# Row operations of a two-block transformer moved to GpSimd, and the planner that orders them

## The chip, the cores and the metric

One core of one Trainium2 chip. The metric is the device time of one execution in microseconds (us), the median of several runs. The engines are TensorE (PE; its weight loads are PEld), VectorE (DVE), ScalarE (ACT), GpSimd (POOL) and SyncE (SP), which issues most of the DMAs.

## What is computed

Two transformer blocks follow one another, on 256 tokens of width 1024, in float32. The first is attention plus an mLSTM and a gated feed-forward layer. The second begins with a layer norm of `x` (gain and bias from `emb_ln_g`, `emb_ln_b`). Its mixer joins two branches, a spatial gating unit and an RWKV-7 recurrence:

```
x = layer_norm(x, emb_ln_g, emb_ln_b)
mod = silu(c) @ w_ada + b_ada            # sh1, sc1, gt1, sh2, sc2, gt2
h = x * (1.0 + sc1) + sh1
p = h @ w_in
u, v = gelu(p[:512]), layer_norm(gelu(p[512:1024]), sg_ln_g, sg_ln_b)
y_a = u * (w_s_masked @ v + b_s)         # the gating
y_b = rwkv7_time_mix(p[1024:], ...)      # two units of four heads here
mix = concat([y_a, y_b]) @ w_out
x = layer_norm(ALPHA * x + gt1 * mix, ln1_g, ln1_b)
h = x * (1.0 + sc2) + sh2                # then a gated feed-forward layer
```

gelu is the tanh form: `0.5 u (1 + tanh(sqrt(2/pi) (u + 0.044715 u^3)))`.

## The kernel before, in words

Tokens lie in two halves of 128 (`b` = 0, 1), features in 8 tiles of 128. A float32 product is made of three matmuls on a high and a low part of each operand: ACT casts a raw weight tile to `whi` and DVE subtracts to give `wlo`. So each weight tile costs one DMA on SP's queue, one ACT and one DVE instruction before PE can use it.

From the first block's output projection on, the order of the instructions on PE, DVE, ACT and POOL is written by a planner (class `Plan`) while the program is built. Each piece of work is a generator (a thread) with a rank; a smaller rank goes first. The planner keeps its own clock with a cost for each instruction (`cost`), and puts the ready instruction of the best rank at the end of its engine's queue. On the chip the queues run in that order: an instruction that waits holds up what stands behind it. Threads wait for named events (`plan.set("m2.1")`, `"base0"`, `"pu1"`, ...). Weights and their matmuls are the thread `stream` of rank 9; a thread of a rank above 9 gets PE only when the stream can't go on, and its instructions on other engines then count as rank 1.

The mixer of the second block, in the order of this argument:

- `chain_ln` makes the mixer's input. After its second half (event `m2.1`) it adds `row_affine`, which multiplies and adds the layer norm's rows to `x`: 2 halves x 2 pieces of 512 x 2 operations, 8 instructions on DVE, on a thread of rank 5. It waits for `r1` (the r data of RWKV unit 1) and sets `m2.x`. The next user of `x` is the residual after the mixer.
- `gmlp` (rank 3) is the gating. It starts at `m2.x`, although its input `v` (event `pv.0`, `pv.1`) is ready early. It runs gelu, layer norm and rows on `v` for both halves, then for each of two pieces of `u` (events `pu0`, `pu1`, the last projections of the stream) gelu, the spatial matmul and the product, and sets `ya`.
- The RWKV units 0 and 1 (ranks 2 and 3) run `rwkv_pre`, `rwkv_gram`, `rwkv_levels`, `rwkv_state`, `rwkv_out` and set `yb0`, `yb1`. Between gram and levels `rwkv_base` (rank 1) solves a 16x16 triangle in 30 small dependent DVE instructions (tile `base`), then goes through DRAM (the `image` tiles), and sets `base0`, `base1`.
- `down_jobs("mix2")`, in the stream, is the output projection: 8 tiles `k`, for both token halves two pieces of three matmuls each, 96 matmuls in all. Tile 0 waits for `ya`, tile 1 for `base0`, tile 4 for `yb0`, tile 6 for `yb1`. Half 1 follows half 0 up to tile 4; its tiles 5, 6 and 7 come at the end.
- `ada` threads compute the modulation vectors. One of rank 10 makes the affine of the feed-forward input (event `aff.f2`); after it `gate`, rank 10, makes the row `gate.mix2` that the residual after `mix2` multiplies with.
- Inverse square roots are a power on GpSimd (`rsq`): one column in layer norms (tile `ln_r`), eight in the RWKV heads (tile `hr_r`, copied by ACT to `rx` and transposed by PE).

All instructions of the planned part are recorded at line 376 of the kernel, where the planner issues them, so the views are read by tile names.

Of the kernel before, what the change touches and what calls it, by code (L numbers as in the profile page):

```python
# [12 lines left out]
AF = mybir.ActivationFunctionType  # L13
ALU = mybir.AluOpType
# [53 lines left out]
class Plan:  # L68
# [210 lines left out]
    def cost(self, x):  # L279

        size = lambda a: a.free_size if isinstance(a.free_size, int) else a.free_size()
        part = lambda a: a.partition_size if isinstance(a.partition_size, int) else a.partition_size()
        aps, kw, op, engine = x.aps, x.kw, x.op, x.engine
        out, n, cost = aps[0], size(aps[0]), 0.06
        x.cols = 0
        if "dma" in op:
            side = aps[0] if aps[0].space != DRAM else aps[1]
            return 1.2 if engine == "gpsimd" else 0.48, part(side) * size(side) * 4 / 360e3
        if op in ("tensor_reduce", "bn_stats"):
            n = size(aps[1])  # L290
        if engine == "tensor":
            cost = 0.002
            k, m, w = P, P, 2 * n
            if op == "matmul":
                k, m = part(kw["lhsT"]), size(kw["lhsT"])
                w = n
                if kw["lhsT"].dtype == F32:
                    w = 4 * n * (0.3 if m <= 32 else 0.55 if kw.get("tile_position") else 1.0)
                    n = max(2.4 * m if kw.get("tile_position") else 4 * m, w)
                else:  # L300
                    n = max(2 * m, n)
            else:
                n *= 2
            x.cols = (w if x.rects[0][0][1] == 0 or m <= 32 else 96) * k / P
        elif engine == "scalar":
            cost = 0.2
        elif engine == "gpsimd":
            cost = 0.44
        elif engine == "vector":
            if op in ("tensor_scalar", "tensor_copy") and all(a.space == out.space != PSUM for a in aps[:2]):  # L310
                n *= 0.5
            if op != "tensor_tensor" and len(aps) > 2:
                cost += 0.06
        return cost, n / RATES[engine]
# [74 lines left out]
class Builder:  # L389
# [665 lines left out]
    def row_affine(self, gb, ev):  # L1055
        for b in range(NB):
            for h in range(2):
                s = slice(h * 512, (h + 1) * 512)
                for i, op in enumerate((ALU.mult, ALU.add)):
                    self.nc.vector.tensor_tensor(self.x[:, b, s], self.x[:, b, s], gb()[i][:, s], op=op)  # L1060
                yield
        self.plan.set(ev)

# [16 lines left out]
    def chain_ln(self, ev, b, residual, hT, nxt, gb):  # L1080

        x = self.x[:, b, :]
        st = self.sm([P, 2, 6], "ln_st")
        yield from residual(ev, b, lambda: self.grow[ev], lambda h, x: self.nc.vector.bn_stats(st[:, h, :], x))
        if hT is None:
            mv, r = self.ln_stats(st)
            sl = [slice(h * 512, (h + 1) * 512) for h in range(2)]
            for s in sl:
                self.nc.vector.scalar_tensor_tensor(x[:, s], x[:, s], mv[:, 0:1], gb()[0][:, s], op0=ALU.subtract, op1=ALU.mult)
            yield GO  # L1090
            for s in sl:
                self.nc.vector.scalar_tensor_tensor(x[:, s], x[:, s], r, gb()[1][:, s], op0=ALU.mult, op1=ALU.add)
                self.nc.sync.dma_start(self.out[0, b * P:(b + 1) * P, s], x[:, s])
                yield GO
            self.plan.set("out.%d" % b)
            return
        half = self.ln_apply(st, x)
        yield "aff." + nxt
        yield from self.to_hT(half, *self.aff[nxt], hT(), b, nxt)
        if b == NB - 1:  # L1100
            self.plan.add(5, self.row_affine(gb, nxt + ".x"), {"m2": "r1"}.get(nxt))


    def ada(self, jobs, pe=False):
# [78 lines left out]
        return [(w, cv, idx * D + h * 512, lambda part, one, h=h: finish(h, part, one)) for h in range(2)]  # L1183

    def gate(self, *args, more=lambda: (), pe=False):
        yield from self.ada(self.ada_gate(*args) + list(more()), pe)

    def ada_affine(self, w, cv, i, b1, j, b2, g, b, ev):

# [584 lines left out]
    def lowrank_jobs(self, w, hT, lr):  # L1774

        nc = self.nc

        def first(sl):
            ps = self.psmm()
            yield from self.feat(ps, 0, sl, hT)  # L1780
            h1 = self.ht("lr1")
            xw, tw = h1[:, 0, :], h1[0:64, 1, :]
            self.shift(xw, ps[:, 0:T], 12)
            nc.scalar.activation(tw, xw[0:64], AF.Tanh)
            lr.extend((xw, tw))
            self.plan.drop(ps)

        def gate(i, n, sl):
            ps = self.psmm()
            yield from self.feat(ps, 0, sl, hT, n)  # L1790
            if n == P:
                lr.append(self.ht("lr2"))
            t = lr[2][0:n, i - 13, :]
            self.shift(t, ps[0:n, 0:T], i, n)
            nc.scalar.activation(t, t, AF.Tanh, scale=0.5)
            nc.vector.tensor_scalar(t, t, 0.5, 0.5, op0=ALU.mult, op1=ALU.add)
            self.plan.drop(ps)
            if n < P:
                self.plan.set("lr")
        return [self.feat_job(None, w, 2560, first), self.feat_job(None, w, 2688, lambda sl: gate(13, P, sl)),  # L1800
                self.feat_job(None, w, 2816, lambda sl: gate(14, 32, sl), cols=32)]
# [429 lines left out]
    def gelu2(self, src, out, t=None):  # L2231

        nc = self.nc
        if t is None:
            t = self.scr.tile([P, 512], F32, tag="res", name="gl_t")
        nc.scalar.activation(t, src, AF.Square)
        nc.vector.tensor_scalar(t, t, 0.044715, 1.0, op0=ALU.mult, op1=ALU.add)
        nc.vector.tensor_tensor(t, t, src, op=ALU.mult)
        yield
        nc.scalar.activation(t, t, AF.Tanh, scale=math.sqrt(2.0 / math.pi))  # L2240
        nc.vector.scalar_tensor_tensor(out, t, 1.0, src, op0=ALU.add, op1=ALU.mult)
        yield
# [195 lines left out]
```

## Time and profile before

| quantity | value |
|---|---|
| time, median of 3 runs | 830.23 us (829.69 to 831.11) |
| the profiled execution: its time | 836.26 us |
| the profiled execution: its span | 834.5 us |
| PE busy | 784.6 us (94%) |
| DVE busy | 581.3 us (70%) |
| ACT busy | 379.8 us (46%) |
| POOL busy | 63.3 us (8%) |

Times in the views are microseconds from the span's start. A busy PE is not PE at its peak: small dependent matmuls count as busy too. PEclk is the granted clock of TensorE as a share of full speed. A tile's row gives count, and minimum, median and maximum duration in ns.

### The profile page before, as it was taken

The numbers are of one execution on the slowest core, as the hardware profiler recorded it, in microseconds if no ns is written. First come the engines' busy times: TensorE is split into PE (matmuls) and PEld (weight loads), VectorE is DVE, ScalarE is ACT, GpSimd is POOL, SyncE is SP. The second block draws the span as 40 slices with busy tenths as digits, with TensorE's granted clock in tenths as the row PEclk, the third lists the DMA queues.
The fourth block names the chain that finished last, engine by engine and source line by source line (L and its number), as shares of the span: only waits on it lengthen the run. The fifth ranks groups of instructions, "written<-read, shape, count | busy, mean of one in ns | idle before, by whom it ended". The sixth has DMA issues, their size and how long they took to land.

```text
span 834.5 us, 14958 instructions
## 1 busy us (share of the span) xinstructions
PE 784.6 (94%) x5912; PEld 674.4 (81%) x5912; DVE 581.3 (70%) x1032; ACT 379.8 (46%) x599; POOL 63.3 (8%) x143
## 2 busy tenths in 40 slices
PE   5999899999979999999998999998897999999995
PEld 4778467899857999998875878876675899999884
DVE  3468866877678977876456467988549778667446
ACT  4346854454554444445425574443235444445330
POOL 3014010100020310000001011000101000000000
PEclk9999999999989999999999999999997999999999
DMA  9996489796759999997659618677434769966711
GB/s 273 318 280 179 159 290 281 208 247 179 245 160 307 272 307 262 305 303 243 186 168 261 165 51 199 155 232 219 153 103 156 219 191 293 251 200 202 254 51 51
DMA packets 205078, 178.94 MB, mean 214 GB/s; under 512 B 24052, under 2 KB 171712, under 8 KB 205008
## 3 DMA queue, kind: packets, MB, share of 16 engines
q1 hardware_dynamic: 201456, 168.37, 69.8%
q0 software_dynamic: 3552, 9.63, 3.5%
q8 instruction: 46, 0.75, 0.4%
q14 instruction: 24, 0.20, 0.1%
HBM read 175.06 MB, written 2.90 MB: 213 GB/s over the span
## 4 chain that ended last, share of the span: by engine, by line
PE 78%; DVE 8%; DMA 5%; ACT 3%; issue 3%; POOL 2%; SPq 1%; DVEq 0%; ACTq 0%; POOLq 0%
PE mm L376 51%; PE sm L376 6%; PE mm L434 4%; PE mm L435 4%; PE mm L436 4%; DMA raw<-in_w_in_dram 2%; PE ad L554 1%; DVE x L376 1%; POOL hr_r L376 1%; DMA base<-image 1%; PE ad L376 1%; DMA ada_raw<-in_w_ada_dram 1%; SPq L376 1%; DMA raw<-in_w_ffn_gate_dram 1%; DVE wlo L376 1%
## 5 line engine op out<-in xcount | busy, mean ns | idle before, releaser
L376 DVE TENSOR_TENSOR wlo<-raw,whi 128x1024 fp32r<-128x1024 f32 (+1 forms) x135 | 164.0, 1218 | 103.2 <-ACT whi L376 102.3
L376 ACT CAST whi<-raw 128x1024 fp32r<-128x1024 f32 (+1 forms) x135 | 140.9, 1045 | 190.3 <-PE mm L376 153.6
L376 PE MATMUL mm<-f_lo,whi 128*128 128x256 f32 x560 | 156.8, 280 | 0.0
L376 PE MATMUL mm<-f_hi,wlo 128*128 128x256 f32 x560 | 156.5, 279 | 0.0
L376 PE MATMUL mm<-f_hi,whi 128*128 128x256 f32 x560 | 156.1, 279 | 0.0
L376 PEld LDWEIGHTS mm<-f_lo,whi 128*128 128x128 f32 x560 | 105.9, 189 | 0.6 <-issue 0.5
L376 PEld LDWEIGHTS mm<-f_hi,whi 128*128 128x128 f32 x560 | 105.5, 188 | 0.3 <-issue 0.2
L376 PEld LDWEIGHTS mm<-f_hi,wlo 128*128 128x128 f32 x560 | 105.2, 188 | 0.7 <-issue 0.7
L427 DVE TENSOR_TENSOR wlo<-raw,whi 128x1024 fp32r<-128x1024 f32 x42 | 51.3, 1220 | 24.2 <-ACT whi L426 24.2
L426 ACT CAST whi<-raw 128x1024 fp32r<-128x1024 f32 x42 | 44.0, 1049 | 45.4 <-DMA raw<-in_w_in_dram 21.1
L434 PE MATMUL mm<-h_hi,whi 128*128 128x256 f32 (+1 forms) x184 | 52.8, 287 | 0.8 <-ACT qkv L1390 0.8
L436 PE MATMUL mm<-h_hi,wlo 128*128 128x256 f32 (+1 forms) x184 | 51.5, 280 | 0.0
L435 PE MATMUL mm<-h_lo,whi 128*128 128x256 f32 (+1 forms) x184 | 51.5, 280 | 0.0
L376 PE MATMUL mm<-m_hi,wlo 128*128 128x256 f32 (+1 forms) x152 | 43.2, 289 | 0.2
L376 PE MATMUL mm<-m_hi,whi 128*128 128x256 f32 (+1 forms) x152 | 42.9, 286 | 0.3 <-DVE kT L376 0.3
L376 PE MATMUL mm<-m_lo,whi 128*128 128x256 f32 (+1 forms) x152 | 42.6, 283 | 0.4 <-DVE vT L376 0.4
L434 PEld LDWEIGHTS mm<-h_hi,whi 128*128 128x128 f32 (+1 forms) x184 | 34.4, 187 | 3.1 <-ACT qkv L1390 1.7
L435 PEld LDWEIGHTS mm<-h_lo,whi 128*128 128x128 f32 (+1 forms) x184 | 34.1, 186 | 0.5 <-issue 0.5
L436 PEld LDWEIGHTS mm<-h_hi,wlo 128*128 128x128 f32 (+1 forms) x184 | 34.2, 186 | 0.0
L376 DVE SCALAR_TENSOR_TENSOR part<-ada_raw,cs,part 128x512 f32<-128x512 f32 x42 | 31.4, 748 | 0.6
L376 PE MATMUL mm<-wlo,hid_hi 128*128 128x512 f32 x80 | 31.3, 391 | 0.0
L376 PE MATMUL mm<-whi,hid_hi 128*128 128x512 f32 x80 | 31.2, 390 | 0.0
(548 smaller groups left out, 1784.0 us busy)
## 6 DMA issues: line engine op xcount, KB each, us to landing
ada_raw<-in_w_ada_dram SPq DMA_DIRECT2D x96, 512.0 KB, 6.0
raw<-in_w_in_dram SPq DMA_DIRECT2D x60, 512.0 KB, 5.4
raw<-in_w_ffn_in_dram SPq DMA_DIRECT2D x44, 512.0 KB, 5.0
raw<-in_w_ffn_gate_dram SPq DMA_DIRECT2D x22, 512.0 KB, 6.0
raw<-in_w_ffn_up_dram SPq DMA_DIRECT2D x22, 512.0 KB, 6.0
raw<-in_w_ffn_down_dram SPq DMA_DIRECT2D x22, 512.0 KB, 5.8
raw<-in_w_ffn_out_dram SPq DMA_DIRECT2D x22, 512.0 KB, 4.1
raw<-in_w_out_dram SPq DMA_DIRECT2D x16, 512.0 KB, 4.3
```

What stands on the lines that cost most here:

```text
L376: return lambda *args, **kw: self.plan.issue(self.name, op, args, kw, lambda: f(*args, **kw))
L426: self.nc.scalar.copy(hi, raw)
L427: self.nc.vector.tensor_tensor(lo, raw, hi.bitcast(F32), op=ALU.subtract)
L434: mm(out, lhsT=l[0], rhs=r[0], start=start, stop=False)
L435: mm(out, lhsT=l[0], rhs=r[1], start=False, stop=False)
L436: mm(out, lhsT=l[1], rhs=r[0], start=False, stop=stop)
L554: nc.tensor.matmul(ps[32 * g:32 * g + 32, :], lhsT=cv["rep"][:, 2 * (s - 1) + g, :], rhs=raws[s - 1 + g // 2][:, g % 2, :], start=s == 1, ...
```

## The change

Five edits. `row_affine` before the mixer (`m2.x`) runs on GpSimd instead of DVE, and starts at `m2.1` instead of `r1`; the gating, which waits for `m2.x`, so starts behind it. The gate's modulation thread takes rank 8.5 instead of 10 once `base0` is set. In gelu, the factor 0.044715 goes into the scale of the ACT square, and the two DVE instructions behind it become one. The planner's cost for GpSimd gets 0.2 us a column for a power, and 2.6 times the element time for other two-input operations.

```diff
         elif engine == "gpsimd":
             cost = 0.44
+            if kw.get("op") == ALU.pow:
+                cost += 0.2 * n
+            elif op == "tensor_tensor":
+                n *= 2.6
@@ row_affine
-                    self.nc.vector.tensor_tensor(self.x[:, b, s], self.x[:, b, s], gb()[i][:, s], op=op)
+                    eng = self.nc.gpsimd if ev == "m2.x" else self.nc.vector
+                    eng.tensor_tensor(self.x[:, b, s], self.x[:, b, s], gb()[i][:, s], op=op)
@@ chain_ln
-            self.plan.add(5, self.row_affine(gb, nxt + ".x"), {"m2": "r1"}.get(nxt))
+            self.plan.add(5, self.row_affine(gb, nxt + ".x"), {"m2": "m2.1"}.get(nxt))
@@ gate
-        yield from self.ada(self.ada_gate(*args) + list(more()), pe)
+        for y in self.ada(self.ada_gate(*args) + list(more()), pe):
+            if pe and "base0" in self.plan.at:
+                self.plan.thread.rank = 8.5
+            yield y
@@ gelu2
-        nc.scalar.activation(t, src, AF.Square)
-        nc.vector.tensor_scalar(t, t, 0.044715, 1.0, op0=ALU.mult, op1=ALU.add)
-        nc.vector.tensor_tensor(t, t, src, op=ALU.mult)
+        nc.scalar.activation(t, src, AF.Square, scale=math.sqrt(0.044715))
+        nc.vector.scalar_tensor_tensor(t, t, 1.0, src, op0=ALU.add, op1=ALU.mult)
```

## Rows read from the trace of the kernel before

**Rows 1.** The page's busy times of the engines, and PE's busy share in 40 equal slices of the span, in tenths.
```profile
PE 784.6 (94%) x5912; PEld 674.4 (81%) x5912; DVE 581.3 (70%) x1032; ACT 379.8 (46%) x599; POOL 63.3 (8%) x143
...
PE   5999899999979999999998999998897999999995
```

**Rows 2.** Busy times by stretch, in the second block's mixer. Columns: stretch, its length, busy time of PE, PEld, DVE, ACT and POOL with instruction counts, granted clock, DMA share, GB/s.
```profile
453.00:470.00 17.00, 17.00 (x116) 15.37 (x115) 6.50 (x8) 7.88 (x12) 0.00 (x0) 1.00 0.73 187
530.00:545.00 15.00, 14.91 (x177) 13.42 (x175) 13.98 (x33) 6.72 (x15) 0.00 (x0) 1.00 0.67 160
545.00:560.00 15.00, 13.93 (x200) 11.81 (x198) 11.98 (x36) 4.43 (x7) 0.03 (x1) 0.89 0.91 275
560.00:575.00 15.00, 11.95 (x205) 9.04 (x205) 13.55 (x33) 5.92 (x11) 1.77 (x3) 1.00 0.65 185
575.00:590.00 15.00, 13.95 (x210) 9.56 (x210) 9.68 (x19) 4.65 (x8) 2.74 (x3) 1.00 0.78 234
630.00:637.00 7.00, 2.13 (x10) 1.60 (x9) 7.00 (x16) 3.86 (x8) 0.56 (x1) 0.68 0.14 25
637.00:643.00 6.00, 6.00 (x18) 4.29 (x19) 5.55 (x11) 3.51 (x7) 2.63 (x3) 0.52 0.81 235
```

**Rows 3.** The chain of work that ended last, in order of time, from unit 1's output to the feed-forward stage. Columns: start, duration, what.
```profile
611.09 1.68 POOL hr_r L376
...
625.38 0.70 DVE res L376
...
636.97 4.05 PE mm L376 x8
```

**Rows 4.** PE alone, the matmuls that read the mixer's output `y_hi` (two of three of the output projection), by stretch.
```profile
590.00:603.00 13.00, 0.73 (x2) 0.87 0.38 141
603.00:619.40 16.40, 10.47 (x32) 1.00 0.21 65
619.40:625.40 6.00, 5.43 (x18) 1.00 0.61 177
625.40:630.40 5.00, 4.14 (x14) 1.00 0.35 102
```

**Rows 5.** The same for `y_lo` (the third), the last two stretches.
```profile
619.40:625.40 6.00, 3.49 (x9) 1.00 0.61 177
625.40:630.40 5.00, 2.72 (x7) 1.00 0.35 102
```

**Rows 6.** Timeline of PE: the end of the projections of `u`, the gate's last matmuls, and two successive matmuls and the last one of the output projection.
```profile
559.78 0.28 PE L376 MATMUL mm<-m_hi,wlo 128*128 128x256 f32 x1
...
591.75 1.13 PE L376 MATMUL adr<-part,sel 128*128 128x512 f32 x2 [0.75 <-ACT part L376]
...
629.53 0.39 PE L376 MATMUL mm<-wlo,y_hi 128*128 128x512 f32 x1
629.76 0.39 PE L376 MATMUL mm<-whi,y_lo 128*128 128x512 f32 x1
```

**Rows 7.** Views by tile: durations (min/median/max ns), first and last start.
```profile
L376 DVE TENSOR_TENSOR x<-x,brow x8: 674/696/704, 529.6 to 547.3; 128x512 f32<-128x512 f32 x8
L376 DVE TENSOR_SCALAR gl_t<-gl_t x4: 417/424/428, 549.3 to 582.3; 128x512 f32<-128x512 f32 x4
```

**Rows 8.** Timeline of DVE. Columns: start, duration, engine, line, operation, tiles, and in brackets idle time before it and its releaser.
```profile
452.69 0.69 DVE L376 TENSOR_TENSOR m_lo<-hf,m_hi 128x512 fp32r<-128x512 f32 x1 [0.32 <-ACT m_hi L376]
...
541.71 1.30 DVE L376 TENSOR_TENSOR x<-x,brow 128x512 f32<-128x512 f32 x2
542.91 0.17 DVE L376 TENSOR_TENSOR base<-base 64x1 f32<-64x1 f32 x1
...
565.80 0.36 DVE L376 COPY base<-base 64x256 f32<-64x256 f32 x1
566.08 0.15 DVE L376 TENSOR_TENSOR f2B<-f2t,f2sh 128x8 f32<-128x8 f32 x1
...
575.34 0.68 DVE L376 TENSOR_TENSOR Lh<-L,half 128x512 f32<-128x512 f32 x1
...
593.58 0.42 DVE L376 TENSOR_TENSOR y_lo<-y,y_hi 128x256 fp32r<-128x256 f32 x1
594.73 0.69 DVE L376 SCALAR_TENSOR_TENSOR y_lo<-gl_t,y_hi 128x512 fp32r<-128x512 f32 x1 [0.74 <-ACT y_hi L376]
...
618.68 0.75 DVE L376 TENSOR_TENSOR y_lo<-y,y_hi 128x256 fp32r<-128x256 f32 x2
```

**Rows 9.** Timeline of POOL: a one-input operation on 512 columns, and powers.
```profile
285.93 0.67 POOL L376 TENSOR_SCALAR_AFFINE_SELECT w_s<-w_s 128x512 f32<-128x512 f32 x1
...
435.40 0.56 POOL L376 TENSOR_TENSOR ln_r<-ln_ve,mhalf 128x1 f32<-128x1 f32 x1 [5.12 <-DVE ln_ve L376]
445.94 1.48 POOL L376 TENSOR_TENSOR ln_r<-ln_ve,mhalf 128x1 f32<-128x1 f32 x1 [3.83 <-DVE ln_ve L376]
489.73 2.60 POOL L376 TENSOR_TENSOR hr_r<-hr_s,mhalf 128x8 f32<-128x8 f32 x1 [41.06 <-DVE rw_D L376]
```

**Rows 10.** Timeline of DVE beside the power at 445.94.
```profile
445.79 1.23 DVE L376 TENSOR_TENSOR wx<-raw,wx 128x1024 fp32r<-128x1024 f32 x1
```

**Rows 11.** Timeline of ACT: the square of the second piece of `u`.
```profile
581.67 0.59 ACT L376 ACTIVATE gl_t<-mm 128x512 f32<-128x512 f32 x1
```

**Rows 12.** Who PE waited for, 453 to 560: us in total, times, longest.
```profile
PE sm L376 <- ACT rx L376: 2.4, 2, 1.6
```

## The prediction

> **What bounds the kernel now.** I read the busy times first: PE is busy for 784.6 of 834.5 us, DVE for 581.3 [rows 1], so PE's stretches with gaps are where time can come from. Then the busy times by stretch [rows 2]: in the second block's mixer PE is full at 453 to 470, but has 3.05 us of gaps at 560 to 575 and 1.05 us at 575 to 590, while DVE is nearly full (13.98 of 15, 13.55 of 15). Behind the mixer, at 630 to 643, PE has a gap of 4.9 us and runs at clocks of 0.68 and 0.52. The chain of waits [rows 3] tells what ends the stage: unit 1's last power on POOL at 611.09, then the output projection up to the first residual at 625.38, then a fixed tail of 11.6 us (residual, layer norm, transposes) to the first feed-forward matmul at 636.97. Behind that PE's slices read 9 to the last one [rows 1], so a shift of the first residual shifts the end one for one.
>
> Now the output projection itself. Hardly any of its 96 matmuls runs before 603: 2 reads of `y_hi` in 590 to 603 [rows 4]. It waits for the gating, `ya`, whose last `y_lo` ends at 595.42 [rows 8]. Unit 1's output is there at 618.68 + 0.75 = 619.43 [rows 8]. After that 18 + 14 + 9 + 7 = 48 matmuls are counted, less two on a boundary 46 [rows 4, 5]. The projection's own order needs only 30 there: 12 of half 0 (tiles 6 and 7) and 18 of half 1 (tiles 5 to 7). So PE still repays work that was held up by the gating.
>
> **The change part by part.**
>
> *Term A, the gating moves ahead.* The `v` part (two gelus, layer norm, rows) leaves 548 to 574 and runs behind 453.4, where the second half of the input is ready [rows 8] and DVE has 10.5 us free in 17 [rows 2]. The `u` part then waits only for its projections, ready at 559.78 + 0.28 = 560.06 [rows 6]. Before, the last piece of `u` took from its square at 581.67 [rows 11] to 595.42, 13.7 us; at that pace `ya` comes at about 574, 21 us earlier. Between there and unit 1's output lie some 40 us, in which tiles 0 to 5 (66 matmuls, 15.2 us at the 0.23 us step of [rows 6]) fill PE's gaps. The 16 surplus matmuls leave the tail: 16 x 0.23 = **3.7 us** gained. Its lower bound is 0 (PE has no room before 619), its upper one 3.7.
>
> *Term B, DVE is freed around unit 1's triangle.* `rwkv_base` of unit 1 runs from 542.91 to 566.16 [rows 8], 23.3 us for small dependent instructions, each of which lets another one between. Of the eight row operations at 0.70 us each [rows 7], three fall into it, the last at 547.3; such instructions follow one another at 0.60 us (two took 1.30 from 541.71 [rows 8]), so that is 1.8 us. The first half of `v` has seven instructions there, five of this size, one of 0.42 and one small, about 3.3 us less the overlaps; the first `u` piece puts five, some 3.0 us, in their place. The fused gelu saves 0.42 us four times [rows 7], of which I count nothing more. Net 1.8 + 3.3 - 3.0 = **2.1 us** gained; bounds 0 (other work fills the places) and 5.1 (the `u` part fits elsewhere).
>
> *Term C, the fill costs the chain.* From 575.34 to 619.43 unit 1 crosses PE about 14 times. A group of three projection matmuls is 0.69 us; a crossing that meets one waits half of it on the mean: 14 x 0.34 = 4.8 us. But the gate's matmuls fill this place already, and the projection does behind 603 [rows 4], so I take a third, **1.6 us** lost; bounds 0 and 4.8 (a whole group each time, 9.7 us, is the rival below).
>
> *Term D, the planner learns what a power takes.* It counted 0.45 us for eight columns where the trace has 2.60 us [rows 9], so the transposes behind it stood too early in PE's queue: PE waited 2.4 us for `rx` in 453 to 560 [rows 12]. With 2.05 us planned, PE gets other work first. Of the 2.4 us much comes before a stretch in which DVE is full, so I take **1.0 us** gained; bounds 0 and 2.4. The same new costs reorder neighbours from the first block on; I count nothing for that and leave 1 us either way in the range.
>
> *The row operations on POOL.* The trace has no multiply or add of two tensors on POOL. A one-input operation on the same 512 columns takes 0.67 us [rows 9]; two reads would be 1.3 us, an estimate from that row; the cost that the change itself writes is 0.44 + 2.6 x 512 / 960 = 1.83 us. I take 1.5 us, 12 us for eight, done at about 465, with ends of 5.4 and 14.6 us. Nothing needs POOL until the power at 489.73 [rows 9]; the gating's row load and powers queue behind and start then. The cover is 36.3 us, 4.5 us an operation; so this costs nothing between those ends. DVE is relieved of 5.6 us.
>
> While a two-input DVE instruction runs, POOL is slower: the one-column power took 0.56 us alone at 435.40, but 1.48 us at 445.94 [rows 9], beside a weight subtraction of 1.23 us from 445.79 [rows 10], and ended 0.40 us after it. In the other direction the subtraction kept its 1.23 us. The Trainium skill (SBUF — State Buffer, section "SBUF: two separate sides") says that whichever of a two-input DVE operation and a GpSimd operation starts first holds their shared port pair for its whole length; this row agrees for DVE in front, and no row has POOL in front with such long operations. By that rule the five weight subtractions at 453 to 470 would each wait for up to one row operation. Worked out from rows, five waits of up to 1.8 us are 9 us against DVE's 10.5 us of room [rows 2], and PE, full there, would lose what its stock of split weights doesn't cover; I bound this by 0 and 2 us and take 0.
>
> *The gate's rank.* The gate's matmuls ended at 592.9 [rows 6], 32 us before the residual. With the projection now competing, its rank above the stream from `base0` on keeps it early. It starts only behind `aff.f2`, at 566.2 [rows 8], whose thread stays at rank 10. I count 0.
>
> Sum: 3.7 + 2.1 - 1.6 + 1.0 = 5.2 us gained, on the profiled execution 836.26 us (its span 834.5 and 1.8 around it), so about 831.1 there. That execution is 6.0 us above the median of the runs; the stage is not special to it, so I take the same 5.2 us off the median: 830.2 - 5.2 = **825.0 us**.
>
> **The rivals.**
>
> *The fill slows the chain (slower).* If each of the 14 crossings waits for a whole group, C is 9.7 us, and if the freed DVE places of B are taken (0) and D is 0, the sum is 3.7 - 9.7 = -6.0, or 836.2; with B at 2.1 it is 834.1. It decides when the crossings lose more than about 6 us together. For it: PE's queue is in order and unit 1 sets the end. Against it: the units' matmuls outrank the stream, so a group is only taken when the planner sees PE idle. I give 12%, centred on 833.
>
> *The gate is late (no change).* The stream, rank 9, can starve `aff.f2`, rank 10, between 574 and `yb0` (593.58 + 0.42 = 594.0 [rows 8]). Before, the gate took 592.9 - 566.2 = 26.7 us behind `aff.f2`; starting at 594 and at the same pace it would be ready at 620.7, just at the new first residual, and the gain would shrink to some 0 to 3 us. Against it: by 560 only a few groups of that thread were left. 11%, about 830.
>
> *GpSimd is slow.* If a row operation took over 4.5 us, the heads' power at 489.73 would wait and `m2.x` come late; at 6 us each the row operations end at 453.4 + 48 = 501.4, 11.7 us too late for unit 0. The rise from 0.56 us for one column to 2.60 us for eight [rows 9] speaks for costs by the column, but it is a power. 5%, 835. Here the change wouldn't do what it says, since the gating would not move ahead. The Trainium skill (GPSIMD Engine Reference, section "Elementwise — side-by-side cycle accounting") has 4497 ns for an addition of 2048 columns; a quarter, 1.1 us, is an estimate from that page, by which the eight take 9 us.
>
> *More is freed.* B at 5.1, C at 0 and D at 2.4 give 11.2 us, 819.0; about 820.5 with part of it. PE's room speaks against it: its gaps from 545 to 590 are 5.2 us [rows 2]. 14%.
>
> **How the numbers follow.** The forecast has the remaining 58%. A measurement of this kernel can tell about 0.2% (1.7 us) from no change. Faster: 55% from the forecast and the 14% of more freed, 69%. Same: 3% from the forecast's edge and the 11% of the late gate, 14%. Slower: 12 + 5 = 17%. The range: below, most of the case of more freed, 820.0; above, A alone against C at 4.8 gives 831.3, with 1 us for reordering and port waits 832.5, which leaves out the slower cases' larger part.
>
> **What would show it.** Right: eight POOL operations on `x` at 453 to 470; `v` done before 500; `ya` at about 574; most reads of `y_hi` before unit 1's last output; about 30 projection matmuls behind it; PE's waits for `rx` near zero; the first residual some 5 us earlier, and the gap to the feed-forward stage still about 11.6 us. Wrong: the first residual waits for the gate's row, unit 1's triangle and levels are as long as before or longer, PE shows gaps ahead of unit 1's output with a lower clock behind them, or weight subtractions are stretched beside the row operations.

## The result, and the profile after

The changed kernel takes 841.82 us (median of 9 runs, 835.80 to 844.37), the kernel before, beside it, 831.2 us. The ratio of their runs is 1.0104, 95% interval 1.0073 to 1.0134: slower by about 8.7 us, where 5.2 us were forecast as a gain. The profiled execution of after took 839.91 us (span 838.0), only 3.65 us more than that of before, since before's profiled execution lies above its median and this one below its own. So the two traces show less than half of these 8.7 us, and the verdicts below are taken from the ratios.

The page's busy times, PE's busy share in 40 slices, and the granted clock:
```profile
PE 785.8 (94%) x5912; PEld 672.7 (80%) x5912; DVE 580.6 (69%) x1020; ACT 379.3 (45%) x599; POOL 75.2 (9%) x151
...
PE   5999899999979999999997999899977999999995
...
PEclk9999999999999999999998999999987999999999
```
Against [rows 1] PE has the same work; POOL has 11.9 us more. For the stage itself I measure from the first normalisation of the mixer's input (436.6 before, 438.4 after; where it starts varies by a few us from one execution to the next, but after also loses 2.85 us ahead of it, which the experiments show) to the first feed-forward matmul. Busy times by stretch, columns as in [rows 2]: first the whole stage, then to the first copy of `v`, to the start of unit 0's triangle, its end, the end of unit 1's, the first residual, the first feed-forward matmul.
```profile
438.40:640.40 202.00, 183.70 (x1760) 145.84 (x1758) 138.38 (x296) 87.96 (x160) 30.70 (x30) 0.95 0.61 166
438.40:467.10 28.70, 23.64 (x162) 13.84 (x161) 21.32 (x32) 10.91 (x21) 16.21 (x16) 0.88 0.83 245
467.10:525.00 57.90, 56.10 (x448) 48.13 (x446) 40.89 (x81) 36.51 (x67) 9.72 (x11) 1.00 0.67 177
525.00:547.60 22.60, 21.43 (x180) 19.62 (x181) 20.15 (x61) 7.26 (x14) 0.00 (x0) 0.92 0.78 202
547.60:575.80 28.20, 27.93 (x409) 24.20 (x407) 22.73 (x60) 13.85 (x26) 0.00 (x0) 1.00 0.61 165
575.80:628.80 53.00, 47.48 (x541) 34.64 (x539) 22.20 (x43) 14.45 (x24) 3.29 (x2) 0.94 0.44 122
628.80:640.40 11.60, 7.12 (x29) 5.41 (x28) 11.08 (x21) 4.97 (x9) 1.47 (x1) 0.79 0.17 47
```
The same milestones of both kernels, in us behind that first normalisation:

| milestone | before | after | difference |
|---|---|---|---|
| first copy of `v` on ACT | 21.8 | 28.6 | +6.8 |
| unit 0's triangle starts | 80.7 | 86.6 | +5.9 |
| unit 1's triangle is done | 129.5 | 137.3 | +7.8 |
| unit 1's output | 182.8 | 186.9 | +4.1 |
| first residual | 188.8 | 190.4 | +1.6 |
| first feed-forward matmul | 200.4 | 202.0 | +1.6 |

So in these two traces after falls behind by 6.8 us before `v` is there, in the first 30 us, and the later stretches give 5.2 of them back; 1.6 us are left in the stage. Timeline of DVE there, and then the end of unit 1's triangle, `ya`, unit 1's output and the first residual:
```profile
449.40 4.05 DVE L380 TENSOR_SCALAR x<-x,ln_mv,ln_r 128x512 f32<-128x512 f32 x2 [0.44 <-POOL ln_r L380]
453.37 1.36 DVE L380 TENSOR_SCALAR hf<-sm,m2A,m2B 128x128 f32<-128x128 f32 x4
455.89 3.52 DVE L380 TENSOR_TENSOR m_lo<-hf,m_hi 128x512 fp32r<-128x512 f32 x2 [1.17 <-ACT m_hi L380]
...
460.72 2.27 DVE L380 TENSOR_TENSOR wlo<-raw,whi 128x1024 fp32r<-128x1024 f32 x1 [1.23 <-ACT whi L380]
466.70 1.23 DVE L380 TENSOR_TENSOR wlo<-raw,whi 128x1024 fp32r<-128x1024 f32 x1 [3.71 <-ACT whi L380]
...
575.40 0.35 DVE L380 COPY base<-base 64x256 f32<-64x256 f32 x1
...
576.40 0.68 DVE L380 SCALAR_TENSOR_TENSOR y_lo<-gl_t,y_hi 128x512 fp32r<-128x512 f32 x1
...
624.54 0.82 DVE L380 TENSOR_TENSOR y_lo<-y,y_hi 128x256 fp32r<-128x256 f32 x2
...
628.80 0.69 DVE L380 TENSOR_TENSOR res<-mm,mix 128x512 f32<-128x512 f32 x1 [3.44 <-PE mm L380]
```
Timeline of POOL: the power of the second half's layer norm, the last of two DMA issues, then the eight row operations, which run from 450.47 to 461.91, beside the stretched DVE rows:
```profile
447.88 1.48 POOL L380 TENSOR_TENSOR ln_r<-ln_ve,mhalf 128x1 f32<-128x1 f32 x1 [3.95 <-DVE ln_ve L380]
...
449.88 0.57 POOL L380 DMA_DIRECT2D lora<-in_b_s_dram  x1
450.47 11.44 POOL L380 TENSOR_TENSOR x<-x,brow 128x512 f32<-128x512 f32 x8
```
The same by tile, 449 to 463 (count, minimum, median and maximum in ns, first and last start):
```profile
L380 POOL TENSOR_TENSOR x<-x,brow x8: 1262/1306/1722, 450.5 to 460.6; 128x512 f32<-128x512 f32 x8
...
L380 DVE TENSOR_SCALAR x<-x,ln_mv,ln_r x2: 1492/2066/2641, 449.4 to 452.0; 128x512 f32<-128x512 f32 x2
```
Timeline of PE: the second half's transposes, a modulation group ahead of that half's projections, and the tail around unit 1's output:
```profile
453.50 0.66 PE L380 MATMUL sm<-ident,x 128*128 128x128 f32 x4 [0.76 <-DVE x L380]
454.09 0.64 PE L380 MATMUL ad<-ada_raw,cs 128*32 128x256 f32 x8
456.75 1.05 PE L380 MATMUL adc<-sel,part 128*128 128x1 f32 x8 [2.02 <-ACT part L380]
457.66 0.48 PE L380 MATMUL mm<-whi,m_hi 128*128 128x512 f32 x1
...
621.38 0.66 PE L380 MATMUL sm<-ident,rx 128*128 128x128 f32 x4 [2.80 <-ACT rx L380]
624.56 0.79 PE L380 MATMUL mm<-whi,y_hi 128*128 128x512 f32 x1 [2.53 <-ACT y_hi L380]
625.15 0.63 PE L380 MATMUL mm<-wlo,y_hi 128*128 128x512 f32 x1
...
629.91 0.40 PE L380 MATMUL mm<-wlo,y_hi 128*128 128x512 f32 x1
```
PE alone, the matmuls that read `y_hi`, behind unit 1's output at 625.36, and then those that read `y_lo`:
```profile
625.36:628.80 3.44, 2.77 (x6) 0.50 0.00 0
628.80:640.43 11.63, 4.56 (x14) 0.79 0.17 46
...
625.36:628.80 3.44, 1.88 (x3) 0.50 0.00 0
628.80:640.43 11.63, 2.77 (x7) 0.79 0.17 46
```
Two things to see. The tail did what term A says: 20 + 10 = 30 projection matmuls are counted behind unit 1's output, less two on a boundary 28 (46 before, counted alike), and the first residual comes 3.4 us behind it, not 6.0. But PE stood still for 2.80 and 2.53 us just ahead, with nothing else in front in its queue, and ten of the matmuls behind that run at 0.63 us in place of 0.39, at a clock of 0.50 (the lower of the two levels, 1.2 GHz). And the second half's input is late: its normalising pair took 4.05 us, and PE then waited 2.02 us for a modulation group.

### The profile page after: what moved, and what is told of

It is laid out like the page before. It is cut to its first block, busy times and chain, and to the rows that moved or that the text cites. A ratio compares the mean times of both kernels' runs of the same rounds, so it can differ in the third digit from the quotient of the medians.

```text
span 838.0 us, 14959 instructions
## 1 busy us (share of the span) xinstructions
PE 785.8 (94%) x5912; PEld 672.7 (80%) x5912; DVE 580.6 (69%) x1020; ACT 379.3 (45%) x599; POOL 75.2 (9%) x151
## 4 chain that ended last, share of the span: by engine, by line
PE 79%; DVE 9%; DMA 5%; issue 3%; ACT 2%; POOL 1%; SPq 0%; DVEq 0%; ACTq 0%; POOLq 0%
PE mm L380 52%; PE sm L380 7%; PE mm L438 4%; PE mm L439 4%; PE mm L440 4%; DVE x L380 2%; DMA raw<-in_w_in_dram 2%; PE ad L380 1%; PE ad L558 1%; DMA base<-image 1%; DMA ada_raw<-in_w_ada_dram 1%; DMA raw<-in_w_ffn_gate_dram 1%; DVE wlo L380 1%; DVE hf L380 1%; PE ad L756 1%
## 5 line engine op out<-in xcount | busy, mean ns | idle before, releaser
L430 ACT CAST whi<-raw 128x1024 fp32r<-128x1024 f32 x42 | 44.1, 1050 | 45.8 <-DMA raw<-in_w_in_dram 21.8
```

The lines of the kernel that those rows point to most:

```text
L430: self.nc.scalar.copy(hi, raw)
```

## The experiments

The first theory: the new planner costs, booked as a gain, are the loss. The second: the row operations on GpSimd hold VectorE up. A third: the planner's order is so sensitive that any edit moves the time, and no edit as such is to blame. Each ratio is to the kernel before, run beside it on the same chip. A table of all runs stands at the end of this section.

**The costs and the row operations, each undone or done alone.** `e1` takes the row operations back to DVE, `e2` the costs back to the old ones, `f1` both; `e3` puts the new costs alone into the kernel before.
```diff
# e1, f1
-                    eng = self.nc.gpsimd if ev == "m2.x" else self.nc.vector
+                    eng = self.nc.vector
# e2, f1 (e3: added to the kernel before)
-            if kw.get("op") == ALU.pow:
-                cost += 0.2 * n
-            elif op == "tensor_tensor":
-                n *= 2.6
```


> The changed kernel, but its eight row operations on DVE again (still from m2.1 on, the gating behind them). Port theory (the row operations on POOL begin while the mixer input's second half is still being normalised and hold up its DVE instructions, 3.0 + 2.2 + 1.0 us in the trace of the changed kernel): the two normalising instructions take 1.0 us again instead of 4.05, the time falls by some 6 us from 841.8 to about 836. Order theory (the planner's new costs for GpSimd make a worse order): 841 to 842, as changed. Gating theory (the earlier gating itself takes DVE from the RWKV units): 841 to 843.

> The changed kernel with the planner's old costs for GpSimd (no 0.2 us a column, no factor 2.6). Port theory: the row operations still hold up DVE, 840 to 842. Order theory: the loss goes, 831 to 834. Gating theory: 840 to 842.

> The kernel before with only the planner's new costs for GpSimd. Port theory: no row operation on POOL, so as before, 830 to 832, or 1 to 2 us better by PE's waits for rx. Order theory: 836 to 842, and the 1.8 us by which the changed kernel is late before the mixer are there too. Gating theory: 830 to 832.

> The changed kernel with the planner's old costs for GpSimd and the row operations on DVE. The kernel with the old costs and the row operations on POOL took 0.9945 of before, and its normalising pair still took 3.2 us instead of 1.0. Port theory: with the rows on DVE the second half is ready 3 to 5 us earlier and the ratio falls to about 0.989 to 0.993, the fastest yet. If DVE's own time counts more than the port (the row operations cost it 4.8 us): 0.995 to 1.000.

Measured: 1.0017 for `e1`, 0.9945 for `e2`, 1.0057 for `e3`, 0.9982 for `f1`. The new costs lose in each of the three pairs: 0.57% on the kernel before, 0.35% with the rows on DVE (`e1` against `f1`), 1.6% with the rows on POOL (after against `e2`). The row operations on POOL lose 0.9% under the new costs (after against `e1`) and gain 0.4% under the old ones (`e2` against `f1`). The intervals overlap at the 0.35% and at the 0.4%, so neither is shown by its pair alone. The two do not look independent at the end, with one order each; up to `v` they are: it comes 3.8 us later with the new costs (25.6 against 21.8 in `e3`, 25.5 against 21.7 in `e1` and `f1`) and 2.7 us later with the rows on POOL (24.4 in `e2`); together 6.5 of the 6.8 us of after.

**Ahead of the mixer, in the same runs.** The new costs change the order from the first block on, and the stage as measured above leaves that out. Timeline of DVE there, from the residual of half 0 to the normalisation of half 1 ahead of the first block's feed-forward layer, before and then after:
```profile
232.59 1.42 DVE L376 SCALAR_TENSOR_TENSOR x<-res,rms_r,x 128x512 f32<-128x512 f32 x2 [0.67 <-POOL rms_r L376]
...
240.60 1.40 DVE L376 SCALAR_TENSOR_TENSOR x<-res,rms_r,x 128x512 f32<-128x512 f32 x2
...
246.05 0.89 DVE L376 TENSOR_SCALAR xn<-x,rms_r 128x512 f32<-128x512 f32 x2 [0.46 <-POOL rms_r L376]
```
```profile
231.28 1.42 DVE L380 SCALAR_TENSOR_TENSOR x<-res,rms_r,x 128x512 f32<-128x512 f32 x2 [0.67 <-POOL rms_r L380]
...
241.97 2.32 DVE L380 SCALAR_TENSOR_TENSOR part<-ada_raw,cols,part 128x512 f32<-128x512 f32 x3
244.21 1.41 DVE L380 SCALAR_TENSOR_TENSOR x<-res,rms_r,x 128x512 f32<-128x512 f32 x2
...
247.60 0.88 DVE L380 TENSOR_SCALAR xn<-x,rms_r 128x512 f32<-128x512 f32 x2 [0.75 <-POOL rms_r L380]
```
This takes 13.46 us in before and 16.32 in after, where the planner put modulation work (`part`) and other instructions ahead of the residual of half 1. All seven kernels with the whole of the new costs (after, `e1`, `e3`, `e4`, `h2`, `k1`, `k4`) have 16.31 or 16.32 us, the other thirteen traces 13.46 or 13.47, `f3` below among them, which leaves out the addition for a one-column power alone. From there to the mixer's first normalisation it is 189.8 to 191.1 us in nineteen of the twenty traces (193.1 in `f4`), so the loss stays. The addition for a one-column power thus loses 2.85 us, 0.34%, whether GpSimd's fixed cost is given as 0.40, 0.44 or 0.48 us: as much as `e1` lies above `f1`, and over half of what `e3` loses.

**Which half GpSimd takes first.** On the chip a queue waits for data, not for the planner's events: the data of half 0 had long been there, and its row operations began as soon as GpSimd's queue came to them, right behind a DMA issue and ahead of the event (`m2.1`) for which the planner had them wait. `e4` lets GpSimd begin with half 1, whose data are ready only later; `f4` does so with the old costs. The order of every queue is the same as in after and in `e2`, so these are tests of the contention alone.
```diff
-        for b in range(NB):
+        for b in ((1, 0) if ev == "m2.x" else range(NB)):
```


> The changed kernel, the row operations taking the second token half first: POOL's queue then can't begin them before that half is normalised and transposed. Port theory: the two normalising instructions take 1.0 us again, the 3 us behind them (m_lo, wlo) stay: 838 to 839. Order theory and gating theory: 841 to 842.

> The changed kernel with the old costs and the row operations taking the second token half first; all queues have the same order as with the old costs alone, only POOL's eight operations work on the halves in the other order. Port theory: the normalising pair takes 1.0 us instead of 3.2, m_lo and wlo are less stretched, 2 to 4 us better than the old costs alone: ratio 0.990 to 0.993. If the stretch is hidden: 0.9945.

Measured: 1.0074 against 1.0104, and 0.9913 against 0.9945: 0.30% and 0.32% less. Timeline of DVE in `e4`, the rows that answer to those of after:
```profile
448.67 1.00 DVE L380 TENSOR_SCALAR x<-x,ln_mv,ln_r 128x512 f32<-128x512 f32 x2 [0.44 <-POOL ln_r L380]
...
452.12 1.05 DVE L380 TENSOR_TENSOR m_lo<-hf,m_hi 128x512 fp32r<-128x512 f32 x1 [0.79 <-ACT m_hi L380]
453.48 1.38 DVE L380 TENSOR_TENSOR m_lo<-hf,m_hi 128x512 fp32r<-128x512 f32 x1 [0.30 <-ACT m_hi L380]
...
458.28 1.38 DVE L380 TENSOR_TENSOR wlo<-raw,whi 128x1024 fp32r<-128x1024 f32 x1 [3.35 <-ACT whi L380]
```
The pair takes 1.00 us again, not 4.05, and the two `m_lo` 1.05 and 1.38, not 3.52 together. So the contention is real. What it costs at the end is less sure: the intervals within a pair overlap, but a third pair, `h1` against `k2` below, has the same sign and size, and the mean of the three, 0.33%, is clear of zero (0.1 to 0.6% with their intervals combined, an estimate). The single pairs give 2.5 to 3.2 us.

**Which of the two costs.** `f3` leaves the addition for a one-column power out, `f2` that for every power (the factor 2.6 stays); `h2` leaves all costs in and only holds the one modulation group that stood ahead of the second half's projections.
```diff
# f3
+                cost += 0.2 * n if n > 1 else 0.0
# f2
-            if kw.get("op") == ALU.pow:
-                cost += 0.2 * n
-            elif op == "tensor_tensor":
+            if kw.get("op") != ALU.pow and op == "tensor_tensor":
# h2: its generator, wrapped
+            def hold(gen):
+                for i, y in enumerate(gen):
+                    yield "m2.1" if i == 10 else y
```


> The changed kernel with the new costs for eight-column powers and for the row operations, but the old cost for one-column powers. In the kernel with only the new costs PE stands 2.0 us before a group adc of the modulation thread (rank 10), which the planner put ahead of the second half's projections, since it took that half to be 0.4 us later. Theory of the one column: the group goes back behind, PE's wait for part falls from 3.0 to 1.0 us or less, the copies of v come some 4 us earlier, and the ratio is about 0.995 to 1.000. Theory of the eight columns or of the factor 2.6: 1.007 to 1.012, as changed.

> The changed kernel with the planner's addition for a power (0.2 us a column) left out; the factor 2.6 on tensor_tensor stays. Theory (the addition for the one-column power shifts TensorE's queue and that is the larger part of the loss; the factor is harmless): about as the kernel with the old costs, ratio 0.993 to 0.999, and TensorE's first adc waits about 1 us for its part, not 2 to 3. Rival (the factor 2.6 is what costs): as the changed kernel, 1.007 to 1.012, with the wait of 2 to 3 us still there. Rival (any number put into the planner moves the order by chance): anything from 0.99 to 1.01, and no relation to that wait.

> The changed kernel, costs and all; only the second group of the final modulation's finish is held until the second half's input is transposed, so that it can't be put ahead of that half's projections. Theory (that place is what the new cost of a power loses): the wait of TensorE's adc falls from 3.0 us to about 1, v comes about 26 us behind the first normalisation in place of 28.7, and the ratio is 1.003 to 1.008. Rival (the loss is spread over the later order, and this place is a symptom): ratio 1.009 to 1.012, with v earlier all the same.

Measured: 1.0019, 1.0026 and 1.0107. Who PE waited for from 435 to 475, in `h2`:
```profile
PE sm L380 <- DVE x L380: 3.6, 2, 2.8
PE adc L380 <- ACT part L380: 1.0, 1, 1.0
```
The wait of `adc` is gone and `v` comes 2.9 us earlier than in after, and yet the time is that of after: unit 0's triangle starts 90.2 us behind the normalisation, in place of 86.6. So my theory that this place is what the costs lose is not borne out; it is one place where they show. The hold also reorders what stands behind it, so what the wait alone costs stays open. `f3` and `f2` are 7.1 and 6.5 us faster than after, and 2.85 us of each is the stretch ahead of the mixer. `f2`, with the wait of `adc` at 1.0, lies 0.8% above `e2` but only 0.1% above `k2` below, the old costs in another order; so it is not shown that the factor on the row operations loses by itself.

**The gate's rank.** `f5` is `e2` with the gate's thread left at rank 10.
```diff
-            if pe and "base0" in self.plan.at:
-                self.plan.thread.rank = 8.5
```


> The changed kernel with the old costs and the gate's modulation left at rank 10. If the higher rank is needed (the rival of the late gate): the gate's row comes after the first residual could start, ratio 0.998 to 1.002. If it is not: within 0.2% of 0.9945.

Measured: 1.0075, against 0.9945 with the rank. It is not the gate that is late (594.7 us in `f5`, 600.1 in `e2`). With the gate's small matmuls out of the way, other groups go to PE inside unit 1's levels and state. From `Lh` to unit 1's last power PE is full in both kernels, but `f5` has 549 matmuls there (59 of the output projection, 17.2 us) where `e2` has 471 (13, 3.8 us), and takes 44.9 us in place of 31.5. Then nothing is left to cover unit 1's end. PE in `f5`, where it waits as in after:
```profile
623.75 1.11 PE L376 MATMUL sm<-ident,rx 128*128 128x128 f32 x4 [2.68 <-ACT rx L376]
627.39 0.79 PE L376 MATMUL mm<-whi,y_hi 128*128 128x512 f32 x1 [2.53 <-ACT y_hi L376]
```

**How far chance of the order goes.** `g1` is the kernel before once more. `g4` gives GpSimd's fixed cost as 0.40 us, not 0.44, in the kernel before; `k1` and `k4` (0.48) do it in the changed kernel; `k2` in `e2`; `h1` and `k3` (0.48) in `f4`. `e8` is the kernel before with the shorter gelu alone.
```diff
# g4, k1, k2, h1; 0.48 in k4, k3
-            cost = 0.44
+            cost = 0.40
# e8
-        nc.scalar.activation(t, src, AF.Square)
-        nc.vector.tensor_scalar(t, t, 0.044715, 1.0, op0=ALU.mult, op1=ALU.add)
-        nc.vector.tensor_tensor(t, t, src, op=ALU.mult)
+        nc.scalar.activation(t, src, AF.Square, scale=math.sqrt(0.044715))
+        nc.vector.scalar_tensor_tensor(t, t, 1.0, src, op0=ALU.add, op1=ALU.mult)
```


> The kernel before, unchanged, for a second trace. Theory (distances between events inside the mixer repeat from one execution to the next, and what varies is when the mixer's normalisation starts): v is 21 to 23 us behind the first normalisation, the first residual 6 us behind unit 1's last output, and the start itself lies within 3 us of the first trace's 436.6. Rival (the distances vary by as much as the change moved them): they differ by over 3 us.

> The kernel before with one number of the planner changed that nothing here calls wrong: GpSimd's fixed cost 0.40 us in place of 0.44. Theory (the power's cost moves the time through one named place, the groups ahead of the second half's projections): ratio 0.998 to 1.002. Rival (the planner's order is so sensitive that any small number moves the time by as much as the new costs did, 0.6 per cent and more): below 0.995 or above 1.005. In that case the verdict on the costs is one on this order alone, and not on whether costs nearer to the chip's are worth having.

> The kernel before with the shorter gelu alone (two VectorE operations in place of three). Theory (it saves some 0.42 us per half row group on VectorE, in stretches where TensorE or ScalarE set the pace): 0.996 to 1.000, the stretch of the feed-forward layers shorter by up to 3 us. Rival (it gives back nothing at all, or moves the order to the worse): 1.000 to 1.004.

> The changed kernel with GpSimd's fixed cost 0.40 us in place of 0.44 in the planner. Theory (the new costs lose by what they are): 1.008 to 1.013 as the changed kernel. Rival (chance of the order): anywhere from 0.99 to 1.015; a result below 1.005 says that the loss of the change is one of this order, not of its costs.

> The changed kernel with the old costs, and GpSimd's fixed cost 0.40 us in place of 0.44. Theory (the rest of the change gains some half per cent by itself): 0.992 to 0.997. Rival (that gain was chance of the order): over 1.000.

> The fastest version so far (old costs, GpSimd begins with the half that VectorE no longer works on; 0.9913), with GpSimd's fixed cost 0.40 us in place of 0.44. If it is robust: 0.988 to 0.997, and some 0.3 per cent below k2_no_costs_040, since the two share an order and differ in the port alone. If it was chance of the order: 0.998 or more.

> The changed kernel with GpSimd's fixed cost 0.48 us in place of 0.44 in the planner. Theory (the new costs lose in any order, by some 1.3 per cent against the old): 1.005 to 1.014. Rival (what was lost is chance of the order): below 1.003. In either case the stretch from the mixer's normalisation to the last layer holds 1,760 matmuls, and its length is TensorE's busy time, which goes by the granted clock, and its idle time: about 200 us with 18 us idle at 0.95, 192 with 13 idle at 0.98.

> The fastest version (old costs, GpSimd begins with the half that VectorE no longer works on) with GpSimd's fixed cost 0.48 us in place of 0.44. Theory (old costs lie lower in any order): 0.990 to 0.999. Rival (0.9913 was one lucky order): 1.000 or more.

Timeline of DVE in `g1`, what before has for the stretched rows of after, and its stage:
```profile
446.02 1.00 DVE L376 TENSOR_SCALAR x<-x,ln_mv,ln_r 128x512 f32<-128x512 f32 x2 [0.44 <-POOL ln_r L376]
...
449.93 0.69 DVE L376 TENSOR_TENSOR m_lo<-hf,m_hi 128x512 fp32r<-128x512 f32 x1 [1.19 <-ACT m_hi L376]
450.94 0.69 DVE L376 TENSOR_TENSOR m_lo<-hf,m_hi 128x512 fp32r<-128x512 f32 x1 [0.32 <-ACT m_hi L376]
```
```profile
435.17:636.16 200.99, 181.18 (x1759) 145.81 (x1758) 138.81 (x310) 88.46 (x160) 18.00 (x22) 0.96 0.59 165
```
Within the stage a kernel repeats: every milestone of `g1` lies within 0.7 us of the first trace, while the stage's start lies 1.4 us earlier. Across orders it does not: a shift of 0.04 us in one cost gave 1.0008 on the kernel before, but 1.0016 in place of 0.9945 (`k2`) and 0.9978 in place of 0.9913 (`h1`). So `k2` came out as its rival says, that the gain of `e2` was chance of the order, and `h1` at the edge of its own; `k1` and `k4` came out as the theory says, `k3` a little faster than that. `e8` has 1 in its interval, so the shorter gelu is not shown to give anything by itself. Three orders each now stand side by side: new costs 1.0132, 1.0104, 1.0078; old costs with half 1 first 0.9978, 0.9913, 0.9895. The two families don't overlap and lie 1.8% apart on the mean, of which 0.3% is the contention (`h1` against `k2`, whose queues are almost the same, gave it a third time, 0.38%). So with the row operations on GpSimd the new costs lose about 1.4%, of which 0.34% lies ahead of the mixer, and up to half a per cent either way is chance of the order. The 0.57% of `e3` is one order and about the size of that chance; of it, only the 2.85 us ahead of the mixer are seen to repeat.

**All runs, and what the stage's length is made of.** The stage holds 1,760 matmuls in every kernel. Its length is PE's busy time, which goes by the granted clock, and PE's idle time. The worst and the best:
```profile
437.63:651.14 213.51, 192.39 (x1760) 153.97 (x1759) 138.78 (x298) 88.35 (x160) 30.14 (x30) 0.90 0.56 155
```
```profile
434.89:623.52 188.63, 176.19 (x1760) 141.86 (x1759) 136.34 (x298) 88.25 (x160) 29.35 (x30) 0.98 0.64 176
```

| kernel | ratio [95%] | `v` behind the start | stage | PE busy | PE idle | clock |
|---|---|---|---|---|---|---|
| before | 1 | 21.8 | 200.4 | 181.6 | 18.8 | 0.96 |
| `g1` before again | - | 21.8 | 201.0 | 181.2 | 19.8 | 0.96 |
| `g4` before, 0.40 | 1.0008 [0.9985, 1.0032] | 21.9 | 199.1 | 179.6 | 19.5 | 0.96 |
| `e8` gelu alone | 0.9980 [0.9956, 1.0004] | 20.4 | 196.6 | 177.8 | 18.8 | 0.98 |
| `e3` costs alone | 1.0057 [1.0030, 1.0084] | 25.6 | 198.7 | 182.9 | 15.8 | 0.94 |
| after | 1.0104 [1.0073, 1.0134] | 28.6 | 202.0 | 183.7 | 18.3 | 0.95 |
| `k1` after, 0.40 | 1.0132 [1.0084, 1.0180] | 29.9 | 213.5 | 192.4 | 21.1 | 0.90 |
| `k4` after, 0.48 | 1.0078 [1.0043, 1.0113] | 25.8 | 200.7 | 183.1 | 17.5 | 0.93 |
| `h2` group held | 1.0107 [1.0069, 1.0144] | 25.7 | 200.3 | 182.7 | 17.6 | 0.95 |
| `e4` half 1 first | 1.0074 [1.0047, 1.0102] | 27.3 | 201.7 | 183.3 | 18.3 | 0.95 |
| `f2` no power cost | 1.0026 [1.0005, 1.0048] | 24.8 | 200.5 | 180.1 | 20.4 | 0.97 |
| `f3` one column old | 1.0019 [0.9992, 1.0047] | 25.6 | 199.1 | 180.8 | 18.2 | 0.95 |
| `e1` rows on DVE | 1.0017 [0.9988, 1.0045] | 25.5 | 195.7 | 181.0 | 14.7 | 0.96 |
| `f1` rows on DVE, old costs | 0.9982 [0.9954, 1.0010] | 21.7 | 197.1 | 182.3 | 14.8 | 0.96 |
| `f5` gate at 10, old costs | 1.0075 [1.0036, 1.0115] | 24.6 | 208.8 | 186.5 | 22.3 | 0.93 |
| `k2` old costs, 0.40 | 1.0016 [0.9992, 1.0040] | 24.8 | 199.9 | 181.6 | 18.4 | 0.95 |
| `e2` old costs | 0.9945 [0.9907, 0.9983] | 24.4 | 191.6 | 178.2 | 13.4 | 0.98 |
| `h1` old, half 1 first, 0.40 | 0.9978 [0.9954, 1.0001] | 21.7 | 197.2 | 181.9 | 15.3 | 0.95 |
| `f4` old, half 1 first | 0.9913 [0.9883, 0.9944] | 21.8 | 190.2 | 179.1 | 11.2 | 0.97 |
| `k3` old, half 1 first, 0.48 | 0.9895 [0.9852, 0.9938] | 21.5 | 188.6 | 176.2 | 12.4 | 0.98 |

Each stage is one trace, and leaves out what lies ahead of it. So ratio and stage don't always rank alike: the traces of `h2`, `k4` and `e3` are of executions below their kernel's median, that of `k1` is of its slowest, both of before lie above theirs, and `e1` and `e3` lose ahead of the stage. What is gained is gained as idle time or as clock: `k3` has 6.4 us less idle than before and 5.4 us less busy time for the same matmuls.

## Why the prediction was wrong, step by step

**Term D, booked as a gain, was the loss; this is the step that failed.** It took costs nearer to the chip's to make a better order, worth 1.0 us, and for "reorder neighbours from the first block on" it counted nothing, with 1 us left either way. PE's waits for `rx` in 453 to 560, from which the 1.0 us came, did go (2.4 us before, none after), but one of 2.80 us stands at unit 1's end instead. And the reordering lost: 2.85 us in the first block in every kernel that has the whole of the new costs, and about 1.4% in all between the two families (0.57%, some 4.7 us, by the costs alone on the kernel before). Why costs that fit the chip better make a worse order is only partly shown. In the first block, the planner takes a one-column power to finish later and puts other DVE work ahead of the residual that waits for it; without that addition (`f3`) the 2.85 us are gone. In the mixer, modulation groups come ahead of the second half's projections in the same way (the wait of 2.02 us; 3.8 us at `v`, in `e3` and in `e1`); but holding that group gave nothing back at the end (`h2`). What else in the order loses is open. The share of chance is shown: half a per cent either way, some 4 us, where the range left 1.

**The port wait, bounded by 0 to 2 us and taken as 0, costs 2.5 to 3.2 us by three pairs.** The bound had the right mechanism and the wrong place. It let the row operations start at 453, behind `m2.1`, and then weighed them against weight subtractions, of which PE has a stock. They started at 450.47, ahead of it, and held up the normalisation and `m_lo` of the second half, which stand on the way to that half's projections: 3.05 us on the pair, 2.1 us on the two `m_lo`. The Trainium skill (SBUF — State Buffer, section "SBUF: two separate sides") says that of a VectorE operation with two inputs in SBUF, or in its two-port mode, and a GpSimd operation the one that starts first holds the pair for its whole length. With POOL in front, which no row of before had, the trace agrees: the second instruction of the pair, begun at 452.0 beside a row operation, took 1.49 us in place of 0.54, and the wait was gone where the two no longer met (`e4`). The first of the pair does not fit: by the records it began 1.07 us ahead of the first row operation and would have ended before it, and yet it took 2.64 us in place of 0.55, in eight traces alike. Why stays open. The prediction weighed that rule and then took 0 against it.

**The row operations' own time** was right: 1.43 us each (11.44 over eight) against 1.5, and POOL was free long before unit 0's power.

**Term A** was right in its mechanism and nearly in its count, 28 matmuls behind unit 1's output where 30 were forecast. `ya` came 20 us earlier behind the stage's start (21 forecast), and the tail became 2.5 us shorter, not 3.7, as PE idled and then ran at the lower clock. What was wrong is the step from there to the end: the matmuls that left the tail are the same PE work elsewhere, and the stage only gets shorter by idle time that they fill. PE's idle time in the stage is 18.3 us, against 18.8 before. `e2` and `f4` are faster than before with a tail as long as its own, 5.8 us and 45 matmuls.

**Term B** is not shown. Unit 1's triangle took 21.5 us (from 554.28) in place of 23.3, near the 2.1 predicted, but the second trace of before (`g1`) has 21.6 us without the change, and the triangle started later. It was not tested alone.

**Term C** did not show: unit 1 took 37.4 us from `Lh` to its output, against 44.1 before, with more projection in between. The gate's rank, counted at 0, is worth 1.3% in one order each (`f5` against `e2`; 0.6% against `k2`, which is within the chance of the order), since without it unit 1's stretch is filled with other matmuls. That is the mechanism of the rival "the fill slows the chain", but in after it is not at work. No rival named the planner's order, and the furthest figure among them, 6.0 us lost (836.2), falls short of the 8.7.

**The rest of the change** gains: with old costs and GpSimd beginning with half 1 it gives 0.9978, 0.9913 and 0.9895, 5.9 us on the mean, where A, B and C sum to 4.2. In the best two, unit 1's output comes earlier (172.9 and 175.4 us behind the normalisation, against 182.8), which the terms did not foresee; so the size agrees better than the way.

## What to carry to other kernels

Moving work within a stage that one engine fills gains only that engine's idle time and clock, so make the sum in these (stage length, busy, idle, clock, before and after), not in how far single events move. A planner's number is part of the program: change it alone, and beside a neutral shift of the same number, before its effect is booked with a sign, and look for its effect from the first instruction that moves, not only in the stage that was meant. Work given to GpSimd runs when its queue comes to it and its data are ready, not when it was planned; give it first what VectorE won't touch soon.

## What the hardware showed that was not expected

GpSimd's row operations stretch VectorE's instructions of both kinds: the pair with one tensor input each from 1.00 to 4.05 us, the two with two inputs from 1.38 to 3.52, a subtraction from 1.23 to 2.27. The four `hf` between them, which read PE's output `sm`, keep their length (1.36 us together beside the same row operations, 1.37 at 449.13 in before). In return they themselves run at 1.26 us at the least and up to 2.3 us beside VectorE's work (the eight took 11.44 us in after, 13.50 in `f4`). And an idle gap was followed by slow matmuls: PE stood for 5.3 us just ahead of the last projection groups, and ten of the matmuls behind that ran at 0.63 us in place of 0.39, at a clock of 0.50.
